# Rotary embedding over split heads: from an fp16 path with casting loads to fp32 in place on three engines

## The chip, the cores and the metric

The kernel runs on one core of a Trainium2 chip. The metric is the device time of one execution in microseconds (us), lower is better; the profile's times are microseconds too unless they are marked ns. The engines are named as in the profile: PE is TensorE (its matrix multiply), PEld its weight load, DVE is VectorE, ACT is ScalarE, POOL is GpSimd, SP is SyncE, which here only issues DMAs.

## The reference

```
x:   (16, 512, 1024) fp32      cos, sin: (512, 32) fp32      num_heads = 16
x = x.reshape(16, 512, 16, 64);  x1, x2 = x[..., :32], x[..., 32:]
out = concat([x1 * cos - x2 * sin,  x1 * sin + x2 * cos], axis=-1)     # cos, sin by position, same for all heads
```

Every output element is one input times a cosine plus the input 32 places away times a signed sine. x is 33.55 MB and the output is 33.55 MB, both fp32.

## The kernel before

A position's row has 1024 elements. A batch of 512 positions is laid on 128 partitions with four consecutive positions each (16 KB of fp32), and two batches make one load.

The load (L84) is issued from the POOL queue, because it converts fp32 to fp16 on the way: x_sb is an fp16 tile of 128 partitions by two batches by 4096 elements. Three such tiles exist (pool xin, bufs=3), so the fourth load waits until VectorE has finished with the first. The loop over bo (L82) runs over 8 loads, the loop over bi (L85) over the two batches in each.

For one batch VectorE makes two fp16 products: A = x times cosine (L90), and Bt = x with the two halves of each head exchanged, times the signed sine (L92). The exchange is an access pattern (swap_view, L75), the sine table carries the minus sign in its first half, and both tables are repeated over the heads by a step of zero. The sum of A and Bt is made by TensorE: for each of 8 pieces of 512 columns, two matmuls with an fp16 identity (L101, L102) add into one fp32 PSUM tile, and ScalarE copies that tile into the fp32 output tile o_sb (L103). A store on SP's queue (L105) writes the 2 MB of one batch. There are three output tiles (pool orez, bufs=3) and four PSUM tiles; A and Bt have two buffers each.

The order on each engine is the program's. What sets the pace around the change are the 16 DMA engines, which serve the POOL queue's loads and SP's stores together, and the buffers, whose release lets the next load or copy begin.

Of the kernel before, what the change touches and what calls it, by code (L numbers as in the profile page):

```python
# [1 line left out]

# [5 lines left out]

FP32 = mybir.dt.float32  # L10
FP16 = mybir.dt.float16
ALU = mybir.AluOpType


@with_exitstack
def kernel(
    ctx: ExitStack,
    tc: tile.TileContext,
    x: bass.AP,
    cos: bass.AP,  # L20
    sin: bass.AP,
    num_heads: bass.AP,
    out: bass.AP,
):
    nc = tc.nc
    P = nc.NUM_PARTITIONS
    batch, seq, dim = x.shape
    nh = num_heads
    head_dim = dim // nh
    half = head_dim // 2  # L30

    KK = seq // P
    assert P * KK == seq
    FREE = KK * dim
    CH = 512
    assert FREE % CH == 0
    BP = 2
    assert batch % BP == 0

    x_v2 = x.rearrange("(bo bi) (p kk) d -> bo p bi kk d", bi=BP, kk=KK)  # L40
    out_v = out.rearrange("b (p kk) h d -> b p kk (h d)", kk=KK)
    cos_v = cos.rearrange("(p kk) j -> p kk j", kk=KK)
    sin_v = sin.rearrange("(p kk) j -> p kk j", kk=KK)

    fixed = ctx.enter_context(tc.tile_pool(name="fixed", bufs=1))
    xin = ctx.enter_context(tc.tile_pool(name="xin", bufs=3))
    tmp = ctx.enter_context(tc.tile_pool(name="tmp", bufs=2))
    orez = ctx.enter_context(tc.tile_pool(name="orez", bufs=3))
    psum = ctx.enter_context(tc.tile_pool(name="psum", bufs=4, space=bass.MemoryType.PSUM))

    ident = fixed.tile([P, P], FP16)
    make_identity(nc, ident)

    cos_sb = fixed.tile([P, KK, half], FP32)
    sin_sb = fixed.tile([P, KK, half], FP32)
    nc.sync.dma_start(out=cos_sb, in_=cos_v)
    nc.sync.dma_start(out=sin_sb, in_=sin_v)
    cos16 = fixed.tile([P, KK, half], FP16)
    sns16 = fixed.tile([P, KK, 2, half], FP16)
    nc.vector.tensor_copy(out=cos16, in_=cos_sb)  # L60
    nc.vector.tensor_scalar_mul(out=sns16[:, :, 0, :], in0=sin_sb, scalar1=-1.0)  # L61
    nc.vector.tensor_copy(out=sns16[:, :, 1, :], in_=sin_sb)  # L62

    cosb = bass.AP(
        tensor=cos16.tensor,
        offset=cos16.offset,
        ap=[cos16.ap[0], [half, KK], [0, nh * 2], [1, half]],
    )
    snsb = bass.AP(
        tensor=sns16.tensor,  # L70
        offset=sns16.offset,
        ap=[sns16.ap[0], [2 * half, KK], [0, nh], [1, 2 * half]],
    )

    def swap_view(x_sb):  # L75
        return bass.AP(
            tensor=x_sb.tensor,
            offset=x_sb.offset + half,
            ap=[x_sb.ap[0], [head_dim, KK * nh], [-half, 2], [1, half]],
        )  # L80

    for bo in range(batch // BP):  # L82
        x_sb = xin.tile([P, BP, KK, dim], FP16)
        nc.gpsimd.dma_start(out=x_sb, in_=x_v2[bo])  # L84
        for bi in range(BP):  # L85
            b = bo * BP + bi
            xb = x_sb[:, bi]

            A = tmp.tile([P, KK, dim], FP16, name="A")
            nc.vector.tensor_tensor(out=A, in0=xb, in1=cosb, op=ALU.mult)  # L90
            Bt = tmp.tile([P, KK, dim], FP16, name="Bt")
            nc.vector.tensor_tensor(out=Bt, in0=swap_view(xb), in1=snsb, op=ALU.mult)  # L92

            o_sb = orez.tile([P, KK, dim], FP32)
            Aflat = A.rearrange("p kk d -> p (kk d)")
            Bflat = Bt.rearrange("p kk d -> p (kk d)")
            oflat = o_sb.rearrange("p kk d -> p (kk d)")
            for c in range(FREE // CH):
                sl = slice(c * CH, (c + 1) * CH)
                ps = psum.tile([P, CH], FP32)  # L100
                nc.tensor.matmul(out=ps, lhsT=ident, rhs=Aflat[:, sl], start=True, stop=False)  # L101
                nc.tensor.matmul(out=ps, lhsT=ident, rhs=Bflat[:, sl], start=False, stop=True)  # L102
                nc.scalar.copy(out=oflat[:, sl], in_=ps)  # L103

            nc.sync.dma_start(out=out_v[b], in_=o_sb)  # L105


# [1 line left out]
_INS = ['x', 'cos', 'sin', 'num_heads']  # L109
_OUTS = [((16, 512, 16, 64), 'float32')]  # L110
#: Inputs that are plain numbers.
_NUMBERS = {'num_heads': 16}


# [26 lines left out]
```

## Time and profile before

| | |
|---|---|
| median of 3 runs | 165.99 us (165.59 to 166.03) |
| span of the profiled execution, first to last instruction | 164.1 us |
| own time of the profiled execution | not recorded apart from its span; the median lies 1.9 us above the span |
| busy: PE, DVE, ACT, POOL | 88.6, 72.5, 68.7, 6.5 us |
| mean granted TensorE clock | 0.767 of full |
| DMA: read from HBM, written to HBM | 33.69 MB, 33.55 MB |
| DMA engines' busy share, by 40 slices | 90% or more in 38 of 40 |
| loads (x8, 4.19 MB read, 2 MB landed each): median issue to landing | 40.3 us |
| stores (x16, 2 MB each): median issue to landing | 23.5 us |

The GB/s figures of the profile count what was landed, so a load that converts fp32 to fp16 counts half of what it reads. A busy engine is not the bound by itself: the question is which wait ends last.

### The profile page before, as it was taken

The page shows a single profiled execution, that of the slowest core. Times are in us where ns is not written, and L with a number is a line of the kernel's source. Part 1 is how long each engine was busy: PE and PEld are TensorE (multiplying, and loading weights), DVE is VectorE, ACT ScalarE, POOL GpSimd, SP SyncE. Part 2 cuts the span into 40 slices and gives each one's busy share as a digit, 9 for nine tenths or more (in the row PEclk, how much of TensorE's full clock was granted, in tenths as well). Part 3 has the DMA queues.
Part 4 walks back from the last instruction along what each step waited for, and adds up shares of the span by engine and source line. Part 5 has one row for each costly group of instructions (what it writes and reads, how often), then busy time and mean ns, then how long its engine had stood idle before and what let it go on. Part 6 is the DMA issues. An engine that isn't in the chain of part 4 may idle for free.

```text
span 164.1 us, 814 instructions
## 1 busy us (share of the span) xinstructions
PE 88.6 (54%) x256; PEld 31.5 (19%) x256; DVE 72.5 (44%) x35; ACT 68.7 (42%) x129; POOL 6.5 (4%) x14
## 2 busy tenths in 40 slices
PE   0000599940954908639195491954919559986000
PEld 0000133310311302213032130311303123331000
DVE  1005979904880073900929037280733707950000
ACT  3000289811805409145080541806428075798100
POOL 7000010010001000010000100000000000000000
PEclk9999999998586585865858658586585855999955
DMA  5999999999999999999999999999999999999992
GB/s 90 196 218 222 220 208 180 290 332 326 312 312 330 324 298 336 306 308 346 310 312 312 326 328 306 326 308 326 326 316 316 304 403 423 413 435 443 423 423 92
DMA packets 4772, 50.51 MB, mean 308 GB/s; under 512 B 416, under 2 KB 672, under 8 KB 672
## 3 DMA queue, kind: packets, MB, share of 16 engines
q0 software_dynamic: 2176, 16.78, 49.7%
q1 hardware_dynamic: 2592, 33.69, 48.8%
q8 instruction: 2, 0.03, 0.1%
q14 instruction: 2, 0.02, 0.0%
HBM read 33.69 MB, written 33.55 MB: 410 GB/s over the span
## 4 chain that ended last, share of the span: by engine, by line
DMA 71%; PE 11%; ACT 6%; DVE 3%; issue 1%; ACTq 0%; POOL 0%; POOLq 0%; DVEq 0%
DMA out_dram<-o_sb 63%; DMA x_sb<-in_x_dram 8%; ACT o_sb L103 6%; PE ps L102 6%; PE ps L101 6%; DVE A L90 1%; DVE Bt L92 1%; ACTq L136 0%; POOL ident masks.py:197 0%; ACTq L103 0%; POOLq masks.py:199 0%; DVEq L90 0%; POOLq L122 0%
## 5 line engine op out<-in xcount | busy, mean ns | idle before, releaser
L103 ACT COPY o_sb<-ps 128x512 f32<-128x512 f32 x128 | 67.4, 609 | 82.9 <-DMA out_dram<-o_sb 58.5
L101 PE MATMUL ps<-A,ident 128*128 128x512 f16 x128 | 65.4, 519 | 60.8 <-ACT o_sb L103 43.6
L90 DVE TENSOR_TENSOR A<-x_sb,cos 128x4096 f16<-128x4096 f16 x16 | 36.7, 2291 | 69.9 <-DMA x_sb<-in_x_dram 41.3
L102 PE MATMUL ps<-Bt,ident 128*128 128x512 f16 x128 | 62.9, 506 | 1.6 <-DVE Bt L92 1.6
L92 DVE TENSOR_TENSOR Bt<-x_sb,sns 128x4096 f16<-128x4096 f16 x16 | 36.6, 2285 | 0.0
L102 PEld LDWEIGHTS <-ident 128*128 128x128 f16 x128 | 15.6, 122 | 87.0 <-issue 83.7
L101 PEld LDWEIGHTS <-ident 128*128 128x128 f16 x128 | 15.8, 124 | 32.1 <-issue 23.5
L84 POOL DMA_DIRECT2D x_sb<-in_x_dram x8 | 5.8, 730 | 83.9 <-DVE Bt L92 83.6
L103 ACT ACT_TABLE_LOAD x1 | 1.3, 1283 | 0.7 <-PEq L122 0.7
L60 DVE CAST cos<-cos_sb 128x128 f16<-128x128 f32 x1 | 0.2, 227 | 2.6 <-DMA cos_sb<-in_cos_dram 2.6
L61 DVE TENSOR_SCALAR sns<-sin_sb 128x128 f16<-128x128 f32 x1 | 0.5, 509 | 0.6 <-DMA sin_sb<-in_sin_dram 0.6
L62 DVE CAST sns<-sin_sb 128x128 f16<-128x128 f32 x1 | 0.4, 434 | 0.0
masks.py:199 POOL TENSOR_SCALAR_AFFINE_SELECT ident<-ident 128x128 f16<-128x128 f16 x1 | 0.3, 304 | 0.1
masks.py:197 POOL MEMSET ident<- 128x128 f16 x1 | 0.2, 205 | 0.3 <-POOLq L122 0.3
L122 POOL MEMSET const-float32-0.0<- 128x1 f32 x1 | 0.1, 93 | 0.2 <-issue 0.2
L122 POOL MEMSET const-bfloat16-1.0<- 128x1 bf16 x1 | 0.1, 95 | 0.0
L122 POOL MEMSET const-uint8-127<- 128x1 uint8 x1 | 0.1, 95 | 0.0
L122 POOL MEMSET const-float32-1.0<- 128x1 f32 x1 | 0.1, 93 | 0.0
## 6 DMA issues: line engine op xcount, KB each, us to landing
out_dram<-o_sb SPq DMA_DIRECT2D x16, 2048.0 KB, 23.5
x_sb<-in_x_dram POOLq DMA_DIRECT2D x8, 2048.0 KB, 40.3
cos_sb<-in_cos_dram SPq DMA_DIRECT2D x1, 64.0 KB, 1.8
sin_sb<-in_sin_dram SPq DMA_DIRECT2D x1, 64.0 KB, 2.2
```

The lines of the kernel that those rows point to most:

```text
L60: nc.vector.tensor_copy(out=cos16, in_=cos_sb)
L61: nc.vector.tensor_scalar_mul(out=sns16[:, :, 0, :], in0=sin_sb, scalar1=-1.0)
L62: nc.vector.tensor_copy(out=sns16[:, :, 1, :], in_=sin_sb)
L84: nc.gpsimd.dma_start(out=x_sb, in_=x_v2[bo])
L90: nc.vector.tensor_tensor(out=A, in0=xb, in1=cosb, op=ALU.mult)
L92: nc.vector.tensor_tensor(out=Bt, in0=swap_view(xb), in1=snsb, op=ALU.mult)
L101: nc.tensor.matmul(out=ps, lhsT=ident, rhs=Aflat[:, sl], start=True, stop=False)
L102: nc.tensor.matmul(out=ps, lhsT=ident, rhs=Bflat[:, sl], start=False, stop=True)
L103: nc.scalar.copy(out=oflat[:, sl], in_=ps)
L122: nc = _bacc.Bacc("TRN2", target_bir_lowering=False, num_devices=1)
```

## The change

Everything is fp32 now, no element is converted. A tile is 128 partitions of 8 consecutive positions (k = 0 to 7), two batches together: 32 KB per partition, one contiguous 4.19 MB in HBM; there are 8 such tiles. x_sb is loaded on SP's hardware queue and its result is written over it and stored from there, also by SP. Five tiles exist (BUFS = 5). The program's order on SP is: loads 0 to 4, stores 0 to 2, loads 5 to 7, stores 3 to 7.

The cosine and the signed sine are put into PSUM once (cos_ps, sns_ps) by three small matmuls that also repeat the 64 partitions' tables for the second batch; sns_sb is a copy of the sines in SBUF for POOL, which does not touch PSUM here.

For each tile (`compute`), by position k:

- k = 0: VectorE makes both products (s0 and, in place, x times cosine); TensorE adds them with an fp32 identity and ScalarE copies the sum back into x_sb.
- k = 1: POOL makes the sine product (s1), VectorE the cosine product in place; TensorE and ScalarE as before.
- k = 2 to 7, two positions at a time: POOL makes the sine product (sp, two buffers), VectorE the cosine product into PSUM (a, one buffer) and then adds sp and a into x_sb.

So a tile has 4 POOL products (one of 1024 elements and three of 2048), 9 VectorE operations (three of 1024 and six of 2048), 8 fp32 matmuls of 512 columns and 2 ScalarE copies of 1024. The order is the one written (manual_schedule).

```diff
-    x_v2 = x.rearrange("(bo bi) (p kk) d -> bo p bi kk d", bi=BP, kk=KK)
-    out_v = out.rearrange("b (p kk) h d -> b p kk (h d)", kk=KK)
+    x_t = x.rearrange("b (s k) d -> (b s) (k d)", k=KK)          # KK = 8
+    o_t = out.rearrange("b (s k) h d -> (b s) (k h d)", k=KK)
...
+    ctx.enter_context(tc.manual_schedule())
...
+    def load(t):
+        x_sb = xin.tile([P, FREE], FP32, name="x_sb")            # BUFS = 5
+        nc.sync.dma_start(out=x_sb, in_=x_t[t * P:(t + 1) * P, :])
+    def store(t):
+        nc.sync.dma_start(out=o_t[t * P:(t + 1) * P, :], in_=xs[t])
...
+    nc.scalar.dma_start(out=tab[:, 0, :], in_=cos_v)
+    nc.scalar.dma_start(out=tab[:, 1, :], in_=sin_v)
+    load(0)
...
-            nc.vector.tensor_tensor(out=A, in0=xb, in1=cosb, op=ALU.mult)
-            nc.vector.tensor_tensor(out=Bt, in0=swap_view(xb), in1=snsb, op=ALU.mult)
-            for c in range(FREE // CH):
-                nc.tensor.matmul(out=ps, lhsT=ident, rhs=Aflat[:, sl], start=True, stop=False)
-                nc.tensor.matmul(out=ps, lhsT=ident, rhs=Bflat[:, sl], start=False, stop=True)
-                nc.scalar.copy(out=oflat[:, sl], in_=ps)
-            nc.sync.dma_start(out=out_v[b], in_=o_sb)
+    def compute(t):
+        nc.gpsimd.tensor_tensor(out=s1, in0=swapped(x_sb, 1, 1), in1=snsb(sns_sb, 1, 1), op=ALU.mult)
+        for k in (2, 4, 6):
+            b = tmp.tile([P, 2 * dim], FP32, name="sp")
+            nc.gpsimd.tensor_tensor(out=b, in0=swapped(x_sb, k, 2), in1=snsb(sns_sb, k, 2), op=ALU.mult)
+        nc.vector.tensor_tensor(out=s0, in0=swapped(x_sb, 0, 1), in1=snsb(sns_ps, 0, 1), op=ALU.mult)
+        nc.vector.tensor_tensor(out=rows(x_sb, 0, 1), in0=rows(x_sb, 0, 1), in1=cosb(0, 1), op=ALU.mult)
+        nc.vector.tensor_tensor(out=rows(x_sb, 1, 1), in0=rows(x_sb, 1, 1), in1=cosb(1, 1), op=ALU.mult)
+        for k, s in ((0, s0), (1, s1)):
+            sm = acc.tile([P, dim], FP32, name="sm")
+            for c in range(0, dim, CH):
+                nc.tensor.matmul(out=sm[:, c:c + CH], lhsT=ident, rhs=x_sb[:, k * dim + c:k * dim + c + CH],
+                                 start=True, stop=False)
+                nc.tensor.matmul(out=sm[:, c:c + CH], lhsT=ident, rhs=s[:, c:c + CH], start=False, stop=True)
+            nc.scalar.copy(out=x_sb[:, k * dim:(k + 1) * dim], in_=sm)
+        for k, b in zip((2, 4, 6), sp):
+            a = acc.tile([P, 2 * dim], FP32, name="a")
+            nc.vector.tensor_tensor(out=a, in0=rows(x_sb, k, 2), in1=cosb(k, 2), op=ALU.mult)
+            nc.vector.tensor_tensor(out=x_sb[:, k * dim:(k + 2) * dim], in0=b, in1=a, op=ALU.add)
+    for n_store in (3, 5):
+        while loaded < NT and loaded < stored + BUFS:
+            load(loaded); loaded += 1
+        for _ in range(n_store):
+            compute(stored); store(stored); stored += 1
```

More of the change, by code (lines that the diff above doesn't have):

```diff
@@ L7 @@
 from concourse._compat import with_exitstack
-from concourse.masks import make_identity
 FP32 = mybir.dt.float32
-FP16 = mybir.dt.float16
 ALU = mybir.AluOpType
+BUFS = 5
+ROUNDS = (3, 5)
 @with_exitstack
@@ L30 @@
     half = head_dim // 2
-    KK = seq // P
-    assert P * KK == seq
+    BP = 2
+    SP = P // BP
+    KK = seq // SP
+    NT = batch // BP
     FREE = KK * dim
     CH = 512
-    assert FREE % CH == 0
-    BP = 2
-    assert batch % BP == 0
-    x_v2 = x.rearrange("(bo bi) (p kk) d -> bo p bi kk d", bi=BP, kk=KK)
-    out_v = out.rearrange("b (p kk) h d -> b p kk (h d)", kk=KK)
-    cos_v = cos.rearrange("(p kk) j -> p kk j", kk=KK)
-    sin_v = sin.rearrange("(p kk) j -> p kk j", kk=KK)
+    assert SP * KK == seq and NT * BP == batch and KK == 8
@@ L45 @@
+    x_t = x.rearrange("b (s k) d -> (b s) (k d)", k=KK)
+    o_t = out.rearrange("b (s k) h d -> (b s) (k h d)", k=KK)
+    cos_v = cos.rearrange("(s k) j -> s (k j)", k=KK)
+    sin_v = sin.rearrange("(s k) j -> s (k j)", k=KK)
     fixed = ctx.enter_context(tc.tile_pool(name="fixed", bufs=1))
-    xin = ctx.enter_context(tc.tile_pool(name="xin", bufs=3))
+    xin = ctx.enter_context(tc.tile_pool(name="xin", bufs=BUFS))
     tmp = ctx.enter_context(tc.tile_pool(name="tmp", bufs=2))
-    orez = ctx.enter_context(tc.tile_pool(name="orez", bufs=3))
@@ L49 @@
[L49 to L97, printed above, removed]
-            for c in range(FREE // CH):
-                sl = slice(c * CH, (c + 1) * CH)
-                ps = psum.tile([P, CH], FP32)
-                nc.tensor.matmul(out=ps, lhsT=ident, rhs=Aflat[:, sl], start=True, stop=False)
-                nc.tensor.matmul(out=ps, lhsT=ident, rhs=Bflat[:, sl], start=False, stop=True)
-                nc.scalar.copy(out=oflat[:, sl], in_=ps)
-            nc.sync.dma_start(out=out_v[b], in_=o_sb)
+    acc = ctx.enter_context(tc.tile_pool(name="acc", bufs=1, space=bass.MemoryType.PSUM))
@@ new lines @@
+    ctx.enter_context(tc.manual_schedule())
+    xs = {}
+    def load(t):
+        x_sb = xin.tile([P, FREE], FP32, name="x_sb")
+        nc.sync.dma_start(out=x_sb, in_=x_t[t * P:(t + 1) * P, :])
+        xs[t] = x_sb
+    def store(t):
+        nc.sync.dma_start(out=o_t[t * P:(t + 1) * P, :], in_=xs[t])
+    tab = fixed.tile([SP, 2, KK * half], FP32, name="tab")
+    nc.scalar.dma_start(out=tab[:, 0, :], in_=cos_v)
+    nc.scalar.dma_start(out=tab[:, 1, :], in_=sin_v)
+    load(0)
+    ident = fixed.tile([P, P], FP32, name="ident")
@@ new lines @@
+    nc.gpsimd.memset(ident, 0.0)
+    nc.gpsimd.affine_select(out=ident, in_=ident, compare_op=ALU.not_equal, fill=1.0,
+                            base=0, pattern=[[-1, P]], channel_multiplier=1)
+    eye2 = fixed.tile([SP, BP, SP], FP32, name="eye2")
+    nc.gpsimd.memset(eye2, 0.0)
+    nc.gpsimd.affine_select(out=eye2, in_=eye2, compare_op=ALU.not_equal, fill=1.0,
+                            base=0, pattern=[[0, BP], [-1, SP]], channel_multiplier=1)
+    neg2 = fixed.tile([SP, BP, SP], FP32, name="neg2")
@@ new lines @@
+    nc.vector.tensor_scalar_mul(out=neg2, in0=eye2, scalar1=-1.0)
+    cos_ps = acc.tile([P, KK, half], FP32, name="cos_ps")
+    sns_ps = acc.tile([P, KK, 2, half], FP32, name="sns_ps")
+    e2 = eye2.rearrange("s b q -> s (b q)")
+    n2 = neg2.rearrange("s b q -> s (b q)")
+    nc.tensor.matmul(out=cos_ps, lhsT=e2, rhs=tab[:, 0, :], start=True, stop=True)
+    nc.tensor.matmul(out=sns_ps[:, :, 0, :], lhsT=n2, rhs=tab[:, 1, :], start=True, stop=True)
+    nc.tensor.matmul(out=sns_ps[:, :, 1, :], lhsT=e2, rhs=tab[:, 1, :], start=True, stop=True)
@@ new lines, with view, rows, swapped @@
+    sns_sb = fixed.tile([P, KK, 2, half], FP32, name="sns_sb")
+    nc.scalar.copy(out=sns_sb, in_=sns_ps)
+    def view(t, offset, dims):
+        return bass.AP(tensor=t.tensor, offset=t.offset + offset, ap=[t.ap[0], *dims])
+    def rows(t, k, n):
+        return view(t, k * dim, [[half, n * nh * 2], [1, half]])
+    def swapped(t, k, n):
+        return view(t, k * dim + half, [[head_dim, n * nh], [-half, 2], [1, half]])
+    def cosb(k, n):
+        return view(cos_ps, k * half, [[half, n], [0, nh * 2], [1, half]])
@@ new lines, in snsb @@
+    def snsb(t, k, n):
+        return view(t, k * 2 * half, [[2 * half, n], [0, nh], [1, 2 * half]])
+    def compute(t):
+        x_sb = xs[t]
+        s1 = tmp.tile([P, dim], FP32, name="s1")
+        nc.gpsimd.tensor_tensor(out=s1, in0=swapped(x_sb, 1, 1), in1=snsb(sns_sb, 1, 1), op=ALU.mult)
+        sp = []
+        for k in (2, 4, 6):
+            b = tmp.tile([P, 2 * dim], FP32, name="sp")
+            nc.gpsimd.tensor_tensor(out=b, in0=swapped(x_sb, k, 2), in1=snsb(sns_sb, k, 2), op=ALU.mult)
+            sp.append(b)
+        s0 = tmp.tile([P, dim], FP32, name="s0")
+        nc.vector.tensor_tensor(out=s0, in0=swapped(x_sb, 0, 1), in1=snsb(sns_ps, 0, 1), op=ALU.mult)
[6 more added lines that the diff above has]
+                                 start=True, stop=False)
+                nc.tensor.matmul(out=sm[:, c:c + CH], lhsT=ident, rhs=s[:, c:c + CH],
+                                 start=False, stop=True)
+            nc.scalar.copy(out=x_sb[:, k * dim:(k + 1) * dim], in_=sm)
[3 more added lines that the diff above has]
+            nc.vector.tensor_tensor(out=x_sb[:, k * dim:(k + 2) * dim], in0=b, in1=a, op=ALU.add)
@@ L109 @@
+    done = stored = 0
+    loaded = 1
+    for n_store in ROUNDS:
+        while loaded < NT and loaded < stored + BUFS:
+            load(loaded)
+            loaded += 1
+        for _ in range(n_store):
+            compute(stored)
+            store(stored)
+            stored += 1
 _INS = ['x', 'cos', 'sin', 'num_heads']
```

## The prediction, made before the changed kernel ran

> **What bounds the kernel now.** I read the page's 40 slices first.
>
> ```profile
> PEclk9999999998586585865858658586585855999955
> DMA  5999999999999999999999999999999999999992
> GB/s 90 196 218 222 220 208 180 290 332 326 312 312 330 324 298 336 306 308 346 310 312 312 326 328 306 326 308 326 326 316 316 304 403 423 413 435 443 423 423 92
> ```
>
> The DMA engines are busy from the second slice to the last but one; no compute engine has such a row. Next I read the totals and the chain of waits.
>
> ```profile
> HBM read 33.69 MB, written 33.55 MB: 410 GB/s over the span
> ...
> DMA 71%; PE 11%; ACT 6%; DVE 3%; issue 1%; ACTq 0%; POOL 0%; POOLq 0%; DVEq 0%
> ```
>
> The chain that ends last is DMA for 71%. Then I cut the span into stretches (length, busy PE, PEld, DVE, ACT, POOL, clock, DMA share, GB/s).
>
> ```profile
> 10.00:14.00 4.00, 0.00 (x0) 0.00 (x0) 0.00 (x0) 0.00 (x0) 0.00 (x0) 1.00 1.06 221
> 40.00:60.00 20.00, 12.67 (x32) 4.37 (x32) 10.01 (x5) 8.59 (x16) 0.72 (x1) 0.66 1.03 320
> 155.00:160.00 5.00, 0.00 (x0) 0.00 (x0) 0.00 (x0) 0.00 (x0) 0.00 (x0) 0.59 1.00 429
> 161.00:162.00 1.00, 0.00 (x0) 0.00 (x0) 0.00 (x0) 0.00 (x0) 0.00 (x0) 0.50 0.16 66
> ```
>
> Stores alone move 429 GB/s. Loads alone land 221, which is 442 read, since a landed fp16 byte is two read bytes. Mixed, 320 landed is about 427 of HBM traffic when reads and writes are equal (each read byte lands as half: 320 / 0.75). So the DMA engines carry 425 to 440 GB/s whatever the mix; I use 430. The kernel is DMA-bound, and its HBM bytes are the reference's own.
>
> **The floor after the change.** HBM bytes stay: 67.2 MB / 0.430 = 156.4 us. Data first moves 1.5 to 2 us into the span, and after the last bytes (about 161.3) 2.8 us pass to the end. Floor: 1.8 + 156.4 + 2.8 = 161.0 us, 3.1 below the span of 164.1. That is all the DMA side can give. Now compute must not be late, and it is three engines' fp32 work on 8 large tiles, with the last store 4.19 MB where it was 2.
>
> **VectorE.** The row and its neighbours in the timeline:
>
> ```profile
> L90 DVE TENSOR_TENSOR A<-x_sb,cos 128x4096 f16<-128x4096 f16 x16 | 36.7, 2291 | 69.9 <-DMA x_sb<-in_x_dram 41.3
> 14.18 2.29 DVE L90 TENSOR_TENSOR A<-x_sb,cos 128x4096 f16<-128x4096 f16 x1 [10.21 <-DMA x_sb<-in_x_dram]
> 16.39 2.29 DVE L92 TENSOR_TENSOR Bt<-x_sb,sns 128x4096 f16<-128x4096 f16 x1
> 16.53 0.59 PE L101 MATMUL ps<-A,ident 128*128 128x512 f16 x1 [16.53 <-DVE A L90]
> ```
>
> 4096 fp16 are 8 KB per operand and partition, as 2048 fp32 are: I take 2.29 us for 2048 fp32 (equal bytes). If it went by elements it would be about 1.2. Two that don't depend on each other start 2.21 apart, 0.08 less than one lasts. One that waits for the other's result starts later: L90 ended at 16.47 and its reader on PE began at 16.53, a hand-off of 0.06. For 1024 elements I use a second point, the cast L60 (128 elements, 227 ns): (2.291 - 0.227) / 1920 = 1.075 ns per element, 0.089 us fixed, so 1.19 us.
>
> The order of instructions with their waits shows cos0 waiting for s0, and each cosine product and addition of k = 2 to 7 for the one ahead, because there is one buffer a. Per tile: s0 to cos0 1.19 + 0.06 = 1.25; the next two 1.10 each; five dependent starts of 2.29 + 0.06 = 2.35, 11.75; the last addition to the next tile's s0 2.21. Sum 17.4 us. Without any price for the waits it is 3 x 1.10 + 6 x 2.21 = 16.6. Each of the nine also reads or writes PSUM, which no VectorE row shows; I bound that by nothing and by the fixed 0.089 once more, 0.8 per tile. ACT's PSUM copies outlast their own spacing by 0.10 (0.59 against 0.49), hardly more than VectorE's 0.08, so I stay nearer to nothing: 0.25. Taken: 17.65 us per tile, bounds 16.6 and 18.2.
>
> [...]
>
> **POOL.** No row shows a product on POOL. Memset 128x1 takes 93 ns and 128x128 205: 0.88 ns per element written. The affine select, one read and one write, takes 304: 1.65 ns per element. A second read at the same price (0.77) would make 2.43. Ends 1.65 and 2.43, I take the middle, 2.04: 7168 elements x 2.04 + 4 x 0.09 = 15.0 us per tile (12.2 to 17.8). It stays under VectorE up to 2.41 ns. POOL also runs at most two sp buffers ahead, which costs nothing while it is the quicker. Only in the first tile does VectorE wait for it: sp of k = 2 is there after 3072 x 2.04 + 0.18 = 6.45 us, a of k = 2 after 5.9, so 0.6 us once.
>
> [...]
>
> **TensorE and ACT.** f16 matmuls of 512 columns start 0.43 apart at half clock and 0.216 at full. fp32 is twice the bytes, so at least 0.43 to 0.86; TensorE's loop is 8 of them, two copies of 1024 (2 x 0.49 + 0.10 = 1.08) and four hand-offs: 8m + 2.4 us, 9.3 at m = 0.86. It decides only from m = 1.9. The copies finish under VectorE's work on k = 2 to 7 (14 us); if that cover went, the excess would fall on each store.
>
> **Loads and the queue.** The conversion on POOL's queue goes; SP issues all x traffic. The first load starts with SP's first DMA at 0.74: cos, 64 KB, was used 1.84 after its issue (2.58), about 1.7 of it fixed. 0.74 + 1.7 + 9.75 (4.194 / 0.430) + 0.3 for the tables: tile 0 at 12.4 (14.18 before, at 12.8 from its issue). Loads 0 to 4 then run to about 51, stores 0 to 2 to 80, loads 5 to 7 to 109, stores 3 to 6 to 148. Load 5 stands behind store 2 on SP, which waits for the third tile (66), and for store 0's landing (61): in time. No tile waits for its load after the first: tile 5 is wanted at 101, landed at 91. The tables' set-up ends long before 12.
>
> **The sum.** 12.4 + 0.6 + 8 x 17.65 = 154.2 for the last tile's end, while the queue has been idle since 148. Then the last store, which nothing covers: 0.75 to the first byte, 9.75, 0.4 for the slowest engine, 2.8 to the end: 13.7. Span 167.9. The median stood 1.9 above the span before: 169.8 us, 2.3% slower. Break-even is 164.1 = 13.0 + 8p + 13.7, p = 17.2 us per tile.
>
> **Rivals.**
> 1. *The floor holds, faster.* If a VectorE tile takes 16.9 or less (waits free, nothing for PSUM), the queue never runs dry and the end is 161.0: 162.9 us. For it: the bound of 16.6. Against it: six of nine operations wait for the one ahead. It decides below 17.2. Chance 0.27, and 0.05 that it lands within 0.3% of 165.99, about what a measurement here can tell from no change.
> 2. *POOL sets the pace.* At 2.43 ns, 17.8 per tile and 1.8 in the first wait, 12.4 + 1.8 + 8 x 17.8 + 13.7 = 170.3, 172.2 us: inside the forecast. At twice the select's price, 3.3 ns, 24.0 per tile: 12.4 + 192 + 2.4 + 13.7 = 220.5, 222 us. The views with runs of 32 are for it, nothing else. Chance of clearly over 17.8: 0.05.
> 3. *TensorE sets the pace.* If an fp32 matmul is four passes, each with its weights (0.12, the rows of PEld) in the open at half clock: 4 x (0.43 + 0.12) = 2.2, 20.0 per tile: 12.4 + 2.4 + 160 + 13.7 = 188.5, 190.4 us. Without the weights it is 1.72, 16.2 per tile, and costs one microsecond at the last store. For it: the clock row falls to 5 between bursts. Chance 0.06.
>
> **How the numbers follow.** VectorE's pace has 0.57: 169.8, its own range 167 to 174 (17.4 with nothing for PSUM: 167.8; 18.2: 174.2). The range of 8 in 10 reaches down to the floor, 162.5, and up to 174.5; it leaves out rivals 2 and 3 (0.11) and the tails. Faster 0.27, same 0.05, slower 0.57 + 0.11 = 0.68.
>
> **What would show it.** Right: the DMA row of the slices has a gap ahead of the last store; the chain of waits runs through DVE L120 to L134 for most of the span; DVE is busy for about 8 x 17; L133 and L134 last 2.3 to 2.4. Wrong: no gap and a span near 161 (L134 starts without the hand-off); VectorE waiting mostly for POOL L116; ACT L130 ending each tile and matmuls of L126 near 2 us.

## The result, and the profile after

The changed kernel takes 175.47 us (median; 175.12 to 175.62) against 165.84 us for the kernel before: a ratio of 1.0586, 95% interval 1.0566 to 1.0605. It is slower, as forecast, but by 5.9% where 2.3% was forecast, and outside the range given. The profiled execution's span is 173.7 us where 167.9 was forecast.

The first view is the page's 40 slices of the changed kernel (each slice 4.34 us), the busy rows of VectorE, GpSimd and the DMA engines.

```profile
DVE  0000579999999999999999989999999999999100
POOL 2000599999999969995999599949995999690000
DMA  7899999998999999298999998998999998850885
GB/s 241 374 420 444 392 453 408 438 475 370 483 392 453 445 400 483 121 483 362 362 483 400 445 475 364 423 415 370 483 392 453 453 392 370 362 242 0 362 362 242
```

DVE is full from the seventh slice on (one 8 in between); before, no compute engine was. The DMA row has the gap ahead of the last store that the prediction named (a 0 between 5 and 8) and a smaller one, the 2 in the seventeenth slice, where the third store waits for its tile. While the queue is full its rate is that of before: 429 GB/s from 20 to 40 us and 431 from 120 to 140, at a DMA share of 1.00. What the forecast did not have is the four zeros at the start of DVE: nearly four slices without arithmetic.

The groups of the changed kernel's page (operation, shapes, count, busy us, mean ns of one, idle time ahead of them and what ended most of it):

```profile
L116 POOL TENSOR_TENSOR sp<-x_sb,sns_sb 128x2048 f32<-128x2048 f32 x24 | 108.2, 4523 | 10.9 <-DVE x_sb L134 10.9
L134 DVE TENSOR_TENSOR x_sb<-sp,a 128x2048 f32<-128x2048 f32 x24 | 54.9, 2288 | 3.9 <-POOL sp L116 1.1
L133 DVE TENSOR_TENSOR a<-x_sb,cos_ps 128x2048 f32<-128x2048 f32 x24 | 55.0, 2294 | 0.6
L130 ACT COPY x_sb<-sm 128x1024 f32<-128x1024 f32 x16 | 16.2, 1012 | 122.9 <-PE sm L128 122.9
L120 DVE TENSOR_TENSOR s<-x_sb,sns_ps 128x1024 f32<-128x1024 f32 x8 | 9.7, 1217 | 17.2 <-ACT sns_sb L91 17.2
```

VectorE's prices are close to those forecast (2.29 and 1.22 us where 2.29 and 1.19 were), and POOL waits for VectorE (10.9 us), VectorE hardly for POOL (1.1). The last row holds the miss: the first product, s0, waited 17.2 us, not for tile 0, which landed at 13.8, but by the profile for sns_sb, the copy of the sines. (s0 itself reads sns_ps, which TensorE finished 0.6 us before that copy ended.) The start of the timeline shows what that copy waited for.

```profile
0.74 0.53 ACTq L67 DMA_DIRECT2D tab<-in_cos_dram  x1
0.74 2.52 SPq L59 DMA_DIRECT2D x_sb<-in_x_dram  x5
1.30 0.61 ACTq L68 DMA_DIRECT2D tab<-in_sin_dram  x1
...
11.19 1.19 PE L87 MATMUL cos_ps<-tab,eye 64*128 64x256 f32 x2 [11.19 <-DMA tab<-in_cos_dram]
...
16.62 1.19 PE L88 MATMUL sns_ps<-tab,neg 64*128 64x256 f32 x2 [4.24 <-DMA tab<-in_sin_dram]
...
18.70 0.59 ACT L91 COPY sns_sb<-sns_ps 128x512 f32<-128x512 f32 x1 [15.47 <-PE sns_ps L89]
19.31 1.22 DVE L120 TENSOR_TENSOR s<-x_sb,sns_ps 128x1024 f32<-128x1024 f32 x1 [17.25 <-ACT sns_sb L91]
```

The two tables, 64 KB each, were issued at 0.74 and 1.30 and used at 11.19 and 16.62: 10.3 and 15.2 us from issue to landing by the page's list of DMA issues, against 1.8 and 2.2 before. From there on the sum holds within 1.5 us. Eight tiles took from 19.31 to 161.47, the end of the last addition, and the last store 12.2 us to the end of the span. The stretches at the end (columns as in the prediction's table) show that store running alone:

```profile
150.00:155.00 5.00, 3.90 (x8) 1.49 (x7) 4.86 (x3) 1.01 (x1) 3.19 (x2) 0.86 0.73 315
155.00:160.00 5.00, 2.36 (x6) 0.76 (x4) 4.86 (x3) 1.01 (x1) 1.64 (x1) 1.00 0.00 0
160.00:162.00 2.00, 0.00 (x0) 0.00 (x0) 1.46 (x1) 0.00 (x0) 0.00 (x0) 0.91 0.00 0
162.00:170.00 8.00, 0.00 (x0) 0.00 (x0) 0.00 (x0) 0.00 (x0) 0.00 (x0) 0.50 1.07 459
```

No byte moves between 155 and 162 while VectorE finishes the last tile. (The last row counts a piece where it starts, so its share is 1.07 and its 459 GB/s too high: by the trace's records of single DMA moves the last store's data moved from 162.4 to 172.3 us, which is about 425 GB/s.) The page's chain of waits is of less use here: it was followed back only to 145, and holds nothing but VectorE's products and additions there.

```profile
DVE 9%; issue 0%; DVEq 0%
DVE x_sb L134 4%; DVE a L133 4%; DVE x_sb L121 1%; DVE x_sb L122 1%; DVEq L134 0%
```

### The profile page after: what moved, and what is told of

It reads as the page before. It is cut to its first block, busy times and chain, and to the rows that moved or that the text cites. A ratio compares the mean times of both kernels' runs of the same rounds, so it can differ in the third digit from the quotient of the medians.

```text
span 173.7 us, 554 instructions
## 1 busy us (share of the span) xinstructions
PE 80.9 (47%) x134; PEld 31.8 (18%) x134; DVE 137.5 (79%) x73; ACT 18.1 (10%) x18; POOL 127.5 (73%) x40
## 5 line engine op out<-in xcount | busy, mean ns | idle before, releaser
L116 POOL TENSOR_TENSOR sp<-x_sb,sns_sb 128x2048 f32<-128x2048 f32 x24 | 108.2, 4523 | 10.9 <-DVE x_sb L134 10.9
L126 PE MATMUL sm<-x_sb,ident 128*128 128x512 f32 x64 | 46.0, 810 | 61.0 <-issue 49.0
L134 DVE TENSOR_TENSOR x_sb<-sp,a 128x2048 f32<-128x2048 f32 x24 | 54.9, 2288 | 3.9 <-POOL sp L116 1.1
L133 DVE TENSOR_TENSOR a<-x_sb,cos_ps 128x2048 f32<-128x2048 f32 x24 | 55.0, 2294 | 0.6
L128 PE MATMUL sm<-s,ident 128*128 128x512 f32 x64 | 40.3, 717 | 0.0
L112 POOL TENSOR_TENSOR s<-x_sb,sns_sb 128x1024 f32<-128x1024 f32 x8 | 18.8, 2350 | 17.6 <-ACT sns_sb L91 17.6
L126 PEld LDWEIGHTS sm<-x_sb,ident 128*128 128x128 f32 x64 | 14.6, 253 | 86.2 <-issue 66.5
L130 ACT COPY x_sb<-sm 128x1024 f32<-128x1024 f32 x16 | 16.2, 1012 | 122.9 <-PE sm L128 122.9
L120 DVE TENSOR_TENSOR s<-x_sb,sns_ps 128x1024 f32<-128x1024 f32 x8 | 9.7, 1217 | 17.2 <-ACT sns_sb L91 17.2
L128 PEld LDWEIGHTS sm<-s,ident 128*128 128x128 f32 x64 | 15.6, 243 | 22.2 <-issue 22.2
L121 DVE TENSOR_TENSOR x_sb<-x_sb,cos_ps 128x1024 f32<-128x1024 f32 x8 | 9.8, 1221 | 0.4
L122 DVE TENSOR_TENSOR x_sb<-x_sb,cos_ps 128x1024 f32<-128x1024 f32 x8 | 9.7, 1216 | 0.0
## 6 DMA issues: line engine op xcount, KB each, us to landing
tab<-in_cos_dram ACTq DMA_DIRECT2D x1, 64.0 KB, 10.3
tab<-in_sin_dram ACTq DMA_DIRECT2D x1, 64.0 KB, 15.2
```

Of the source, the lines that this page charges most:

```text
L112: nc.gpsimd.tensor_tensor(out=s1, in0=swapped(x_sb, 1, 1), in1=snsb(sns_sb, 1, 1), op=ALU.mult)
L116: nc.gpsimd.tensor_tensor(out=b, in0=swapped(x_sb, k, 2), in1=snsb(sns_sb, k, 2), op=ALU.mult)
L120: nc.vector.tensor_tensor(out=s0, in0=swapped(x_sb, 0, 1), in1=snsb(sns_ps, 0, 1), op=ALU.mult)
L121: nc.vector.tensor_tensor(out=rows(x_sb, 0, 1), in0=rows(x_sb, 0, 1), in1=cosb(0, 1), op=ALU.mult)
L122: nc.vector.tensor_tensor(out=rows(x_sb, 1, 1), in0=rows(x_sb, 1, 1), in1=cosb(1, 1), op=ALU.mult)
L126: nc.tensor.matmul(out=sm[:, c:c + CH], lhsT=ident, rhs=x_sb[:, k * dim + c:k * dim + c + CH], start=True, stop=False)
```

## The experiments

The theory: the tables share the 16 DMA engines with five loads of x in runs of 32 KB. (A run is the contiguous piece that an engine moves at a time, here one partition's row of a DMA: the changed kernel's trace has 2048 moves of 32 KB for its 16 DMAs of 128 rows.) A table has 64 runs of 1 KB, four for each engine, and if an engine serves the two queues in turn, each small run waits while one large run passes: 32 KB at 430 / 16 = 26.9 GB/s is 1.22 us. The rivals: the pace or the end costs the time and the late start is hidden; ACT's queue is itself slow; the engines share by bytes. e2, e3, e4 and e8 are one execution each, the others medians of 4 to 10.

**e1, the tables ahead.** Both tables are issued by SP ahead of load 0, so no x runs beside them.

```diff
-    nc.scalar.dma_start(out=tab[:, 0, :], in_=cos_v)
-    nc.scalar.dma_start(out=tab[:, 1, :], in_=sin_v)
+    nc.sync.dma_start(out=tab[:, 0, :], in_=cos_v)
+    nc.sync.dma_start(out=tab[:, 1, :], in_=sin_v)
     load(0)
```

> Edit: both table loads on SP's queue, ahead of load 0. Theory: the late start comes from the tables alone, which share each DMA engine with 32 KB runs of x and get one small run in per big one. Then they land by about 3 us, VectorE's first product starts when tile 0 has landed (12.4 to 13.0 instead of 19.3), everything behind shifts by 6.3 to 6.9: span 166.8 to 167.4, time 168.5 to 169.3. The pace per tile stays at 17.56. Rival (the pace of the engines or the store at the end costs the time, the late start is hidden): span stays near 173.7, time 175.5.

Measured: 170.88 us, ratio to the kernel before 1.0316 (1.0299 to 1.0334), span 169.0. From its timeline:

```profile
1.97 2.60 SPq L59 DMA_DIRECT2D x_sb<-in_x_dram  x5
3.02 1.19 PE L87 MATMUL cos_ps<-tab,eye 64*128 64x256 f32 x2 [3.02 <-DMA tab<-in_cos_dram]
...
14.63 1.22 DVE L120 TENSOR_TENSOR s<-x_sb,sns_ps 128x1024 f32<-128x1024 f32 x1 [12.56 <-DMA x_sb<-in_x_dram]
```

The tables land at 2.9 and 3.5, the first product waits for tile 0 alone, and the span falls by the same 4.7 us by which the first product moved (19.31 to 14.63): nothing hid the late start. But tile 0 came at 14.6, not at 12.4 to 13.0. Two issues of 0.55 us and more stand ahead on SP, so load 0 is issued at 1.97, and the first product follows 12.7 us later, where the expectation had 11.7. The kernel before had shown this: its first load took 12.8 us from issue, with 9.75 for the bytes.

**e2, the tables on ACT's queue without company.** Loads 0 to 4 go behind the tables on that queue.

```diff
-        nc.sync.dma_start(out=x_sb, in_=x_t[t * P:(t + 1) * P, :])
+        eng = nc.scalar if t < BUFS else nc.sync
+        eng.dma_start(out=x_sb, in_=x_t[t * P:(t + 1) * P, :])
```

> Edit: the tables stay where they were, on ACT's queue, and loads 0 to 4 are put behind them on the same queue, so nothing runs beside the tables. Theory (sharing with the large runs): tables land within 3 us, first product at 12.5 to 14, span 167 to 168. Rival (ACT's queue is itself slow, or the activation table's load of 1.28 us holds it up): tables land after 10 and 15 us as before, and the span is 173.7 or more.

Measured: 170.76 us, span 168.8; the tables land 2.1 and 2.3 us after their issue and the first product is at 14.48. ACT's queue is not slow; the span stands 0.8 above what was expected, for the reason of e1.

**e3, half the runs of x.** Each load of x becomes two DMAs of 16 KB runs, tables beside them as in the change.

```diff
-        nc.sync.dma_start(out=x_sb, in_=x_t[t * P:(t + 1) * P, :])
+        for h in range(0, FREE, FREE // 2):
+            nc.sync.dma_start(out=x_sb[:, h:h + FREE // 2], in_=x_t[t * P:(t + 1) * P, h:h + FREE // 2])
```

> Edit: each load of x is cut into two DMAs of 16 KB runs; tables as they were, on ACT's queue beside them. If a table's run waits for one run of x per turn, the turn halves: cos lands about 6 us after its issue instead of 10.3, sin about 8.5 instead of 15.2, before tile 0, and the first product starts at 12.5 to 13.5: span 167 to 168. If the engines share by bytes or time, cutting the runs changes nothing: 10.3, 15.2, 173.7.

Measured: 170.12 us, span 168.3; cos lands after 7.8 us and sin after 10.0, the first product is at 14.16. Halving the runs takes 2.5 us off the first table and 5.2 off the second. At 0.61 us saved per large run that is 4.1 and 8.5 turns: a table has 4 runs per engine, both have 8. The turn goes by runs, not by bytes. The tables still landed later than the 6 and 8.5 us expected: the turns halved, but the wait before a table's first run did not (see the end of the next section).

**e4, twice as many table runs.** The same tables in four DMAs with runs of 512 B.

```diff
-    nc.scalar.dma_start(out=tab[:, 0, :], in_=cos_v)
-    nc.scalar.dma_start(out=tab[:, 1, :], in_=sin_v)
+    hw = KK * half // 2
+    for i, v in ((0, cos_v), (1, sin_v)):
+        for h in range(0, 2 * hw, hw):
+            nc.scalar.dma_start(out=tab[:, i, h:h + hw], in_=v[:, h:h + hw])
```

> Edit: each table is loaded by two DMAs of half the columns: the same bytes in twice as many runs of 512 B. If each small run waits for a turn behind a 32 KB run, the second sin half lands after some 25 to 28 us instead of 15.2, the first product starts at 28 to 31, and the span is 182 to 186. If it goes by bytes, nothing changes: 173.7.

Measured: 187.0 us, span 185.1; the last half of sin lands 25.1 us after its issue, the first product is at 30.56. This is the second dose in the other direction, and the span follows the first product once more (11.3 and 11.4 us more than after the change).

The trace's records of single DMA moves show the turns one by one. Of the changed kernel's page, this line is ACT's queue: 128 runs of 1 KB, and 32 pieces of 4 bytes, the markers that end a table's share on each engine.

```profile
q10 hardware_dynamic: 160, 0.13, 0.2%
```

The four runs of cos start on the 16 engines at 4.8 to 5.4, 6.1 to 6.6, 7.4 to 7.9 and 8.7 to 9.2 us, and its markers at 10.0 to 10.6. These turns are 1.3 apart, which is one run of x (1.21 to 1.27) and one of the table (0.05). In e3 they are 0.65 to 0.7 apart. So a table takes five turns on each engine, four runs and a marker.

**e5, the last store in pieces.** e1, and the last tile stored in four pieces as they are done.

```diff
-            store(stored)
+            if stored < NT - 1:
+                store(stored)
+            else:
+                for k in (2, 4, 0, 6):
+                    nc.sync.dma_start(out=o_t[stored * P:(stored + 1) * P, k * dim:(k + 2) * dim],
+                                      in_=xs[stored][:, k * dim:(k + 2) * dim])
```

> Edit: the tables ahead on SP's queue, as in e1, and the last tile stored in four pieces of two positions (k = 2, 4, 0, 6), each as soon as it is done. In e1 VectorE ended at 156.8 and the span at 169.0: 12.2 us, of which some 9.2 are the uncovered 4.19 MB. Theory: three quarters of the last store move under the last tile's work, 6.9 us: span 162, time 164. Rival (the queue is not free before the last tile's end, or 8 KB runs are slower): less than half of it, span 165 or more, time 167 or more.

Measured: 164.51 us, ratio 0.994 (0.9921 to 0.9959), span 162.6: 6.4 us less than e1. The uncovered last store cost that, and without it and the late tables the fp32 kernel is a little faster than the one before, by 0.6%. The slices of e5 show the gap closed:

```profile
DVE  0004979999999999999999989999999999999950
DMA  5889989989999998999999989999999999999994
```

**e7, a shorter tile for VectorE.** e1 with the sum of k = 2 given to TensorE and ScalarE as well.

```diff
-        for k in (2, 4, 6):
+        for k, n in ((3, 2), (5, 2), (7, 1)):           # s1 and VectorE's third product now hold k = 1 and 2
...
-        for k, s in ((0, s0), (1, s1)):
+        for k, s, o in ((0, s0, 0), (1, s1, 0), (2, s1, dim)):
```

> Edit: the tables ahead as in e1, and one more position's sum (k = 2) given to TensorE and ScalarE: POOL makes the sine products of k = 1, 2 in one operation, then 3-4, 5-6 and 7; VectorE loses one addition of 1024 per tile. Theory (VectorE's pace sets the end): a tile takes 16.3 to 16.5 instead of 17.56, POOL's 15.9 just under it, the last tile ends 8 to 9 us sooner than in e1, at 148, and the DMA queue is about to become the bound: span 161 to 162.5, time 163 to 164.5. Rival (POOL's pace, or the hand-over of its two buffers): 17 or more per tile, time 168 or more.

Measured: 165.21 us, ratio 0.9964 (0.995 to 0.9978), span 163.3. VectorE's last addition ends at 149.25 where e1's ended at 156.77: 0.94 us less per tile, so VectorE's pace did set the end in e1. The span gained 5.7 of those 7.5 us. Its last store left SP only at 151.3, 2 us behind VectorE: TensorE's and ScalarE's share of the tile now ended last, a cover that the expectation had not counted.

**e6, both ends in pieces.** e5, and tile 0 loaded in four pieces with 8 KB runs.

```diff
+        n = 2 * dim if t == 0 else FREE
+        for h in range(0, FREE, n):
+            nc.sync.dma_start(out=x_sb[:, h:h + n], in_=x_t[t * P:(t + 1) * P, h:h + n])
```

> Edit: e5, and tile 0 loaded in four pieces of two positions with 8 KB runs, so that its arithmetic begins when the first has landed. First product at 7 to 8 us instead of 14.6; the last tile ends at about 150 and the DMA queue is never empty before it. Theory (then the DMA engines are the bound, at 425 to 430 GB/s): span 161 to 162, time 163 to 164. If the floor of 161.0 is wrong and the queue can go faster, span 155 to 158; if the small runs cost, 164 or more.

Measured: 164.53 us, ratio 0.993 (0.9909 to 0.9951), span 163.0. The first product came at 7.23 and the last addition ended at 149.05, 7.6 us sooner than in e5, and the span did not move. The DMA engines are the bound:

```profile
60.00:100.00 40.00, 21.71 (x34) 8.68 (x35) 39.08 (x23) 4.05 (x4) 34.20 (x9) 0.76 1.00 432
100.00:150.00 50.00, 27.45 (x47) 10.40 (x46) 47.73 (x24) 6.07 (x6) 41.11 (x11) 0.81 1.00 430
150.00:158.00 8.00, 0.00 (x0) 0.00 (x0) 0.00 (x0) 0.00 (x0) 0.00 (x0) 0.50 0.99 418
```

(The columns are those of the prediction's table of stretches.) The DMA share is 1.00 at 430 to 432 GB/s and runs on at 0.99 after the arithmetic has ended. The span lies 2 us above the floor of 161.0, and 1 above what was expected. Most of it is that no byte of x moves until the two table issues are past: by the DMA records x's first run starts at 3.2, where it started at 1.8 after the change. The small runs are not it, since e10 has the same and reaches 161.1.

**e9, the same with a shorter tile.** e6 with the edit of e7.

> Edit: e6 with the sum of a third position on TensorE and ScalarE, as in e7: the arithmetic now needs 16.5 us per tile in place of 17.56. Theory (e6 is at the floor of the DMA engines): no gain, span 162.5 to 163.3, time within 0.3 per cent of e6. Rival (VectorE's pace still sets the end in e6): the span falls by up to 8 us.

Measured: 165.02 us, span 163.0, and VectorE done at 146.15, 2.9 us sooner than in e6, for nothing. That confirms e6's bound.

**e10, tables beside small runs.** e6 with the tables back on ACT's queue, as in the change.

> Edit: the tables back on ACT's queue, beside the loads as in the changed kernel; tile 0 in four pieces with 8 KB runs and the last store in four pieces, as in e6. Theory (a table's run waits for one run of x per turn): with 32, 16 KB runs cos landed 10.3, 7.8 us after its issue and sin 15.2, 10.0; at 8 KB about 6.5 and 7.4. First product at 10.5 to 11.5, last tile ended at 153, and x flows 1.2 us sooner than in e6, whose two table issues stood ahead on SP: the DMA engines are the bound and the span is 161.5 to 162.3, time 163.0 to 163.8. If the share does not go by runs: sin after 13 or more, first product after 17, span 165 or more.

Measured: 163.17 us (163.11 to 163.22), ratio 0.9848 (0.9832 to 0.9865), span 161.1. The tables land 5.1 and 7.5 us after their issue: sin lies on the line of the other two run lengths, cos 1.4 us below it. The first product is at 11.62, and x flows from the start. This is the fastest version of the study, 1.5% below the kernel before, and its span is the floor worked out beforehand. That the two agree to 0.1 is partly luck: the data of x and the output moved for 158.0 us (1.8 to 159.8) where 156.4 were reckoned, and 1.3 us followed it where 2.8 were. In its slices (4.03 us each) VectorE starts in the third, and the DMA row is full from the second to the last but one, as it was before the change:

```profile
DVE  0019799999999999999999999999999999999900
DMA  5999999999999999999999999999999999999993
```

**e8, the cosines from SBUF.** The changed kernel, but VectorE reads the cosines from a copy in SBUF, so that five of its operations per tile have both inputs there. No other run has such operations beside POOL's products.

```diff
+    cos_sb = fixed.tile([P, KK, half], FP32, name="cos_sb")
+    nc.scalar.copy(out=cos_sb, in_=cos_ps)
...
-        return view(cos_ps, k * half, [[half, n], [0, nh * 2], [1, half]])
+        return view(cos_sb, k * half, [[half, n], [0, nh * 2], [1, half]])
```

> Edit: the changed kernel, but VectorE reads the cosines from a copy in SBUF instead of from PSUM, so five of its nine operations per tile have both inputs in SBUF; nothing else. [...]

Measured: 249.91 us, span 248.0. Its groups:

```profile
L118 POOL TENSOR_TENSOR sp<-x_sb,sns_sb 128x2048 f32<-128x2048 f32 x24 | 133.5, 5577 | 45.0 <-DVE x_sb L136 45.0
L124 DVE TENSOR_TENSOR x_sb<-x_sb,cos_sb 128x1024 f32<-128x1024 f32 x8 | 44.2, 5526 | 0.0
L123 DVE TENSOR_TENSOR x_sb<-x_sb,cos_sb 128x1024 f32<-128x1024 f32 x8 | 31.3, 3913 | 0.5
```

The same products of 1024 that took 1.22 us with a PSUM operand take 3.9 and 5.5 on average while POOL works, and POOL's take 5.6 instead of 4.5. In the trace, VectorE's product of 54.48 to 60.00 ends 1.1 us after the POOL product beside it, 53.44 to 58.92: by these times it waited for the whole of the other. At 64.64 it is the other way round: VectorE's product takes 2.30 us, and the POOL product that begins 0.04 us behind it takes 6.62, 2.1 more than its 4.52 after the change. Where POOL stands still, the 2048 product from SBUF takes 2.29 us, as with PSUM:

```profile
59.92 2.29 DVE L135 TENSOR_TENSOR a<-x_sb,cos_sb 128x2048 f32<-128x2048 f32 x1
```

So a PSUM operand costs VectorE nothing here (2.294 us with it, 2.29 without), and it keeps the two engines apart: after the change, VectorE's products of 1024 took 1.21 to 1.22 us in all eight tiles, and POOL's of 2048 took 4.50 to 4.54.

## Why the prediction was right on the pace and wrong on the start

The span of 173.7 is 5.8 above 167.9. In the prediction's own terms:

- *Tile 0 at 12.4*: the first product was at 19.31, +6.9. This is the step that failed. The sentence "The tables' set-up ends long before 12" and the 0.3 us for the tables priced them by their bytes and by how they had landed before (1.8 and 2.2 us), where by the DMA records the first run of x started only at 2.8, after cos had landed, and not beside 32 KB runs already under way. e1 to e4 and e10 show what took its place: a table's run passes once per run of x, and the tables landed 10.3 and 15.2 us after their issue. Without it, the start would still have been late: the first product came 12.7 us after load 0's issue (e1), which gives 13.4 for an issue at 0.74, 1.0 more than forecast (whose own terms add up to 12.5). The row of before, 12.8 from issue, stood in the same sentence and was replaced by a sum of 430 GB/s and a fixed 1.7 that leaves the slow start out: the first run on each engine took 1.5 to 2.3 us, later ones 1.21. The remaining 5.9 are the tables.
- *0.6 + 8 x 17.65 = 141.8*: measured 142.2. The pace is right: with hand-offs of 0.03 to 0.11 us in the dependent starts and nothing for PSUM a tile takes 17.6 (tile 7 began at 143.76, tile 6 at 126.14). That it agrees so closely is partly luck: the 0.25 for PSUM was not there, and the starts lay 0.2 further apart per tile than the 17.4 of the sum without it. The bound of 16.6 fell, since the waits do cost.
- *POOL at 2.04 ns per element, 15.0 per tile*: measured 4.523 us for 2048 (2.21 ns per element), 15.9 per tile with its 2.35 for 1024. It cost some 0.4 us, in the first tile's wait of 1.06 where 0.6 was forecast. POOL stayed under VectorE as forecast.
- *PSUM operand, 0.25 per tile*: none was found (2.294 with, 2.29 without, in e8).
- *TensorE, 8m + 2.4*: m was twice the 0.43 to 0.86 of that term, as rival 3 had it without the weights, and below the 1.9 from which it decides. In the last tile's burst the matmuls start 1.71 us apart while the granted clock is 0.50 (146 to 150 us) and 0.86 apart while it is 1.00 (from 154), two of the trace's records to each; that is four times the f16 spacing of 0.43 and 0.216 before. ACT's second copy there ended at 158.4, 3 us ahead of VectorE. Rival 3 did not occur.
- *The last store, 13.7*: measured 12.2, -1.5. Its first byte came 0.9 us after VectorE's last addition, where 0.75 was put; its data took 9.9 us, as priced; 1.4 us passed from its last byte to the end, where 0.4 and 2.8 were put. The kernel before shows why: most of its engines were done by 161.3, from which the 2.8 were counted, but its slowest only at 162.5, so that engine was priced twice.
- *Median above span, 1.9*: 1.8.

Sum: 6.9 + 0.4 - 1.5 = 5.8. Rival 1, the floor, was right as a place: e6 and e10 reach 163.0 and 161.1. The prediction had asked for a VectorE below 17.2 us per tile; at 17.56 the arithmetic fits under the DMA's time as soon as it starts at 11.6 and its last store is in pieces. A quicker VectorE comes near it as well: in e7, at 16.5 us in most tiles and with the last store whole, the span was 163.3.

One thing stays open. Of cos's 10.3 us the four turns from its first run to its marker explain 5.3, and 0.4 pass from the last marker to the landing. The rest is the wait for the first run, which starts at 4.8 to 5.4 us where it starts at 2.1 in e1. After the change two runs of x pass on each engine before it, but the wait does not go by runs: the first table run starts at 4.7 to 4.9 beside runs of 32, 16 and 8 KB alike (the changed kernel, e3, e4, e10). In e8, with the same loads and tables as the changed kernel, it starts at 6.1, and the tables take 11.3 and 16.0 us. What holds it is not shown.

## What to carry to other kernels

A small load that everything waits for is not priced by its bytes once it shares the DMA engines with long runs: count its runs per engine, add one for the marker, and multiply by the time of one run of the other queue (five turns of 1.3 us here, 0.65 to 0.7 in e3); here some 4 us before its first run came on top. Or issue it ahead, or keep the first other runs short. When a DMA-bound kernel gets larger tiles, price its two ends before its middle: the first tile's landing and the last tile's store stand uncovered. Cutting the last store took 6.4 us off e1 here, a shorter tile 5.7 (e7); cutting the first load as well brought nothing (e6 against e5) until the tables no longer stood ahead of it on SP (e10, 1.4 us by the medians). Where VectorE and GpSimd worked side by side, an operand of VectorE in PSUM is what kept them from stopping each other (1.22 us for 1024 with it, up to 5.5 without).

## What the hardware showed that was not expected

- A 64 KB load of 1 KB runs took 10.3 to 16.0 us beside 32 KB runs, 7.8 to 10.0 beside 16 KB, 5.1 to 7.5 beside 8 KB, and 2.1 to 2.3 alone.
- A VectorE product of 1024 with both inputs in SBUF took up to 5.5 us beside GpSimd products, 1.22 with one in PSUM.
- Issuing a 64 KB load took SP 0.55 us, and nothing behind it left sooner: two of them ahead of the first large load moved the end by the 1.4 us between the medians of e6 and e10.
